# Attention in a decoder trunk: 64 by 64 products for the dilated groups, their weights transposed on TensorE, and a head's values ahead of the next head's scores

## The chip, the core and the metric

The kernel runs on one core of one Trainium2 chip. The metric is the time of one execution on the device in microseconds (us), the median of several runs. The engines are called as in the profile: PE is TensorE (its weight loads are PEld), DVE is VectorE, ACT is ScalarE, POOL is GpSimd, SP is SyncE, which issues most of the loads. PSUM is the memory that PE writes its products to.

## The reference, cut to what matters

A trunk of two layers over 256 tokens of width 1024: layer 0 mixes with a gated short convolution, layer 1 with dilated attention; each is followed by a squared-ReLU MLP (4096 wide) and a gated embedding. The change is in the attention of layer 1 alone.

```python
DILATED_PATTERNS = ((128, 1), (512, 4), (2048, 16))   # window, dilation: groups 0, 1, 2

def dilated_attention_mixer(h, positions, w_qkv, w_o):
    b_, s_, _ = h.shape
    g_, hh, dh = N_ATTN_GROUPS, ATTN_HEADS_PER_GROUP, ATTN_HEAD_DIM   # 3, 8, 128
    qkv = (h @ w_qkv).reshape(b_, s_, 3, g_ * hh, dh)
    q = partial_rotary(qkv[:, :, 0], positions).reshape(b_, s_, g_, hh, dh)
    k = partial_rotary(qkv[:, :, 1], positions).reshape(b_, s_, g_, hh, dh)
    v = qkv[:, :, 2].reshape(b_, s_, g_, hh, dh)
    outs, lses = [], []
    for g, (window, dilation) in enumerate(DILATED_PATTERNS):
        o_g, lse_g = dilated_window_attention(q[:, :, g], k[:, :, g], v[:, :, g], window, dilation)
        outs.append(o_g)
        lses.append(lse_g)
    weights = jax.nn.softmax(jnp.stack(lses, axis=0), axis=0)
    o = jnp.sum(weights[..., None] * jnp.stack(outs, axis=0), axis=0)
    return o.reshape(b_, s_, hh * dh).astype(h.dtype) @ w_o
```

A query of group g sees the keys at most `window` back whose distance is a multiple of `dilation`, itself among them. Weighting the three groups by the softmax of their log-sums is the same as one softmax over the keys of all three groups together, and so the kernel computes it: one row of scores for each query, over the keys of group 0, 1 and 2.

## The kernel before, in words

The program is a list (`make_plan`, line 139) of products and steps, and TensorE's work is issued in the order of that list. A product is one 128-row piece of a weight matrix against the activations; weights come from memory in slabs of up to eight 128 by 128 pieces, and each slab is split into two parts (`whi` on ACT, line 357; `wlo` on DVE, by the helper of line 296), since every product of f32 values is made of three products of rounded ones (`fp32r`). Slabs are split up to five ahead of their use. All products of weights run in `block` (line 393).

The 256 tokens stand in the order of `residue_order` in layer 1: token t at (t mod 4) * 64 and on, so that each run of 64 holds the tokens of one remainder by 4, and inside it runs of 16 hold those of one remainder by 16. Groups 1 (dilation 4) and 2 (dilation 16) therefore only have valid pairs inside a run of 64. A block b is 128 tokens, two such runs.

For each head h of 8, the plan has the products of q and k for the three groups (`qk`, eight k each), with their sums (`add_up`) and rotation (`qk_out`, on POOL for all but the first head's groups), then the products of v for all three groups (`v`, eight k). Between these stand the steps of the head before, in `make_plan` at lines 199 to 206: `scores` after `qk(h, 0)`, `turn` after `qk(h, 2)`, `values` after six of eight k of `v(h)`. For head 0 (`late`) they stand one place later. After the last head, lines 208 to 216 put its three steps between the products of `w_o`, of which k = 0 to 7 stand for the heads' outputs.

- `scores` (line 674): for each block, group 0 as three rounded products over all 256 keys (line 681), groups 1 and 2 each as one plain f32 product of the block's 128 queries with its own 128 keys (line 684). The row of 512 scores is masked and its maximum taken on DVE (line 687), and made into weights on ACT (lines 691, 693).
- `turn` (line 695): the weights must stand with the keys in the partitions. Group 0's 256 columns are transposed on TensorE (line 708), then split in two parts. Those of groups 1 and 2 are transposed on DVE in blocks of 32 by 32: the blocks on the diagonal in one go (line 701), their neighbours within a run of 64 in four more (line 704).
- `v_out` (line 662): the values leave PSUM scaled: group 0 in two parts (lines 668, 669), groups 1 and 2 in one copy of 256 columns (line 670) into `v12`.
- `values` (line 711): group 0 as six rounded products (line 718), then groups 1 and 2 as one plain f32 product for each block and group (line 724), all added into one PSUM bank of 128 by 256; the output is split in two parts (lines 735, 736).

PSUM tiles come from one pool of eight buffers (`bank`, or a `psum.tile` directly); the activations of this stage come from the pools `act` (13 buffers) and `pair` (20).

Of the kernel before, what the change touches and what calls it, by code (L numbers as in the profile page):

```python
# [15 lines left out]
P = 128  # L16
S = 256
# [121 lines left out]
def make_plan():  # L139
# [27 lines left out]
    def mix(key, j, ks):  # L167
        return [("n", key, k, 2 * j + i, ("o", j), i, "y") for k in ks for i in (0, 1)]
# [9 lines left out]
    def qk(h, g, ks):  # L178
        return [
            ("w" if h else "n", "qkv", k, (i, g, h), ("qk", h, g), i, "x3") for k in ks for i in (0, 1)  # L180
        ]

    def v(h, ks):
        return [("t", "v", k, h, ("v", b, h), b, "x3") for k in ks for b in (0, 1)]
# [11 lines left out]
    def sums(h, g):  # L196
        return [("do", "add_up", ("qk", h, g)), ("do", "qk_out", h, g)]

    for h in range(1, HEADS):

        late, steps = h == 1, [[("do", what, h - 1)] for what in ("scores", "turn", "values")]
        plan += qk(h, 0, range(NK)) + ([("do", "values", 0)] if h == 2 else []) + sums(h, 0)
        plan += [("do", "qk_split", 0)] if late else steps[0]
        plan += qk(h, 1, range(NK)) + sums(h, 1) + qk(h, 2, range(NK)) + steps[late ^ 1] + sums(h, 2)
        plan += v(h, range(3)) + [("do", "qk_split", h)] + v(h, range(3, 6)) + steps[2 - late]
        plan += v(h, range(6, NK)) + [("do", "v_out", h)]

    last = HEADS - 1
    plan += [x for k in (0, 1, 2) for j in range(NP) for x in mix("w_o", j, (k,))]
    plan.append(("do", "scores", last))  # L210
    plan += [x for k in (3, 4) for j in range(NP) for x in mix("w_o", j, (k,))]
    plan.append(("do", "turn", last))
    plan += [x for j in range(NP) for x in mix("w_o", j, (5,))]
    plan.append(("do", "values", last))
# [40 lines left out]
def tile_trunk(ctx: ExitStack, tc: tile.TileContext, plan, slabs, ap, out):  # L255
# [36 lines left out]
    def flat(t):  # L292
        return t.rearrange("p i s -> p (i s)")
# [285 lines left out]

    def masks_load():  # L580
        for b in (0, 1):
            mask[b] = apool.tile([P, 512], F32, tag="act", name=f"mask{b}")
            nc.sync.dma_start(mask[b], ap["mask"][:, b, :])

    def conv(c):
# [75 lines left out]

    def v_out(head):

        v0, v12 = act(f"v0_{head}", F32R), act(f"v12_{head}")
        for b in (0, 1):
            p, r = flat(close(("v", b, head))), rstd[3][:, b : b + 1]
            hi, lo = v0[:, b, :P], v0[:, b, P:]
            nc.scalar.activation(hi, p[:, :P], AF.Copy, scale=r)
            nc.vector.scalar_tensor_tensor(lo, p[:, :P], r, f32(hi), ALU.mult, ALU.subtract)
            nc.scalar.activation(v12[:, b, :], p[:, P : GROUPS * P], AF.Copy, scale=r)  # L670
        cur["v", head] = v0, v12


    def scores(head):
        weights = cur["pr", head] = pair(f"sm{head}", dtype=F32)[2]
        for b in (0, 1):
            own = slice(b * P, (b + 1) * P)
            ps = psum.tile([P, 512], F32, tag="ps", name=f"sc{head}_{b}")
            hi, lo, _ = state["qk"][head]
            for n, (q, k) in enumerate(((hi, hi), (hi, lo), (lo, hi))):  # L680
                nc.tensor.matmul(ps[:, :S], q[:, 0, own], k[:, 1, :], start=n == 0, stop=n == 2)  # L681
            for g in (1, 2):
                t = cur["qk", head, g]
                nc.tensor.matmul(ps[:, (g + 1) * P : (g + 2) * P], t[:, 0, own], t[:, 1, own], start=True, stop=True)  # L684
            sm = flat(weights[:, b])
            stats = [spool.tile([P, 1], F32, tag=f"st{n}_{b}", name=f"st{n}_{head}_{b}") for n in range(3)]
            nc.vector.tensor_tensor_reduce(
                out=sm, in0=ps, in1=mask[b], op0=ALU.add, op1=ALU.max, scale=SCALE, scalar=NEG, accum_out=stats[0]
            )
            nc.vector.tensor_scalar(stats[1], stats[0], -1.0, None, ALU.mult)  # L690
            nc.scalar.activation(sm, sm, AF.Exp, bias=stats[1], accum_out=stats[2])
            nc.vector.reciprocal(stats[2], stats[2])
            nc.scalar.activation(sm, sm, AF.Copy, scale=stats[2])

    def turn(head):

        sm = cur.pop(("pr", head))
        t = cur["pT12", head] = act(f"pT12_{head}")  # L700
        nc.vector.transpose(t, sm[:, :, 1, :])
        for q in range(4):
            rows, cols = (slice(n * 32, (n + 1) * 32) for n in (q, q ^ 1))
            nc.vector.transpose(t[cols, :, rows], sm[rows, :, 1, cols])
        ps = bank(f"tp{head}")
        for b in (0, 1):
            for n in (0, 1):
                nc.tensor.transpose(ps[:, n, b * P : (b + 1) * P], sm[:, b, 0, n * P : (n + 1) * P], ident)
        split_into("pT", head, ps)

    def values(head):
        ps = bank(f"o{head}")
        v0, v12 = cur.pop(("v", head))
        hi, lo, _ = state["pT"].pop(head)
        for kb in (0, 1):
            vhi, vlo = v0[:, kb, :P], v0[:, kb, P:]
            for n, (a, b) in enumerate(((vhi, hi), (vhi, lo), (vlo, hi))):
                nc.tensor.matmul(  # L718
                    ps[:, 0, :], a, b[:, kb, :], start=kb == 0 and n == 0, stop=False, skip_group_check=True
                )  # L720
        t = cur.pop(("pT12", head))
        for b in (0, 1):
            for g in (0, 1):
                nc.tensor.matmul(  # L724
                    ps[:, 0, b * P : (b + 1) * P],
                    v12[:, b, g * P : (g + 1) * P],
                    t[:, b, g * P : (g + 1) * P],
                    start=False,
                    stop=g == 1,
                    skip_group_check=True,  # L730
                )
        if head % 2 == 0:
            state["y"][head // 2] = pair(f"y{head // 2}")
        hi, lo = (t[:, head % 2, :] for t in state["y"][head // 2][:2])
        nc.scalar.activation(hi, ps[:, 0, :], AF.Copy)
        nc.vector.tensor_tensor(lo, ps[:, 0, :], f32(hi), ALU.subtract)
# [116 lines left out]
def masks():  # L853

    import numpy as np

    t = np.argsort([residue_order(t) for t in range(S)])
    m = np.full((P, 2, 512), NEG, np.float32)
    for b in range(2):
        q = t[b * P : (b + 1) * P, None]  # L860
        for keys, to, window, step in (
            (t, slice(0, S), 128, 1),
            (t[b * P : (b + 1) * P], slice(S, S + P), 512, 4),
            (t[b * P : (b + 1) * P], slice(S + P, S + 2 * P), 2048, 16),
        ):
            d = q - keys[None]
            m[:, b, to][(d >= 0) & (d <= window) & (d % step == 0)] = 0.0
    return m


# [56 lines left out]
```

## Time and profile before

| | |
|---|---|
| median of 3 runs | 777.29 us (777.19 to 777.32) |
| the profiled execution | 777.36 us, its span 775.5 us |
| granted TensorE clock, mean | 0.998 |
| first to last `scores` (start of line 684) | 349.6 to 543.3 us of the span |
| last `values` (start of line 724) | 554.0 us |

The span is the time from the first to the last instruction in the trace; some 1.9 us of the execution lie around it. In the profile's page the busy times count each engine by itself. Matmuls overlap, so that a busy PE says that something was always under way, not how much fits in. Rows of a timeline give the start, the time from the first start to the last end, engine, line, operation, tiles, shape (stationary rows*columns, then the moving operand) and the count. Rows of one tile give the shortest, median and longest duration in nanoseconds. Rows of waits give the one that waited, the one it waited for, the sum in us, how often and the longest.

### The profile page before, as it was taken

The numbers are of one execution on the slowest core, as the hardware profiler recorded it, in microseconds if no ns is written. First come the engines' busy times: TensorE is split into PE (matmuls) and PEld (weight loads), VectorE is DVE, ScalarE is ACT, GpSimd is POOL, SyncE is SP. The second block draws the span as 40 slices with busy tenths as digits, with TensorE's granted clock in tenths as the row PEclk, the third lists the DMA queues.
The fourth block names the chain that finished last, engine by engine and source line by source line (L and its number), as shares of the span: only waits on it lengthen the run. The fifth ranks groups of instructions, "written<-read, shape, count | busy, mean of one in ns | idle before, by whom it ended". The sixth has DMA issues, their size and how long they took to land.

```text
span 775.5 us, 12403 instructions
## 1 busy us (share of the span) xinstructions
PE 766.9 (99%) x4780; PEld 696.3 (90%) x4780; DVE 595.5 (77%) x863; ACT 439.4 (57%) x677; POOL 167.1 (22%) x110
## 2 busy tenths in 40 slices
PE   9999999999999999999999999999999999999996
PEld 8998998888888899989999989989988888888885
DVE  6898779898566668789789889887798887555664
ACT  7655565565444446557655655655665555444454
POOL 0000000000000000078867867865000000000002
PEclk9999999999999999999999999999999999999999
DMA  8965655655565554654546445456465655555521
GB/s 313 301 192 187 187 184 180 195 187 191 190 188 190 191 190 138 210 182 157 170 150 183 158 152 188 150 161 208 135 211 181 190 188 188 188 188 191 190 93 54
DMA packets 42538, 140.95 MB, mean 182 GB/s; under 512 B 4848, under 2 KB 6128, under 8 KB 42480
## 3 DMA queue, kind: packets, MB, share of 16 engines
q1 hardware_dynamic: 41904, 139.52, 55.9%
q8 instruction: 37, 0.61, 0.3%
q10 hardware_dynamic: 576, 0.66, 0.3%
q14 instruction: 21, 0.17, 0.1%
HBM read 139.10 MB, written 1.05 MB: 181 GB/s over the span
## 4 chain that ended last, share of the span: by engine, by line
PE 97%; issue 1%; DMA 1%; DVE 0%; POOL 0%; SPq 0%; POOLq 0%; DVEq 0%; ACT 0%
PE acc_u L393 23%; PE acc_d L393 23%; PE acc_qk L393 17%; PE acc_v L393 9%; PE acc_o L393 6%; PE acc_g L393 5%; PE acc_B L393 3%; PE acc_C L393 3%; PE acc_X L393 3%; PE o L724 1%; PE sc L684 1%; PE acc_p L393 1%; PE o L718 1%; PE sc L681 1%; DMA pt<-in_pT 1%
## 5 line engine op out<-in xcount | busy, mean ns | idle before, releaser
L296 DVE TENSOR_TENSOR wlo<-raw,whi 128x1024 fp32r<-128x1024 f32 (+2 forms) x277 | 353.2, 1280 | 125.6 <-ACT whi L357 122.7
L357 ACT ACTIVATE whi<-raw 128x1024 fp32r<-128x1024 f32 (+2 forms) x277 | 278.2, 1007 | 214.3 <-PE acc_d L393 77.1
L393 PE MATMUL acc_d<-u,whi 128*128 128x512 f32 x512 | 160.8, 395 | 0.0
L393 PE MATMUL acc_u<-x,whi 128*128 128x512 f32 x512 | 160.8, 395 | 0.0
L393 PE MATMUL acc_qk<-x,whi 128*128 128x512 f32 (+1 forms) x432 | 134.5, 368 | 0.0
L393 PEld LDWEIGHTS acc_d<-u,wlo 128*128 128x128 f32 x512 | 96.2, 188 | 22.7
L393 PEld LDWEIGHTS acc_u<-x,wlo 128*128 128x128 f32 x512 | 96.2, 188 | 22.5
L463 POOL TENSOR_TENSOR n<-v,power 128x2 f32<-128x2 f32 (+1 forms) x6 | 3.9, 650 | 517.1 <-DVE v L488 512.6
L393 PE MATMUL acc_qk<-x,wlo 128*128 128x256 f32 x384 | 108.0, 281 | 0.0
L393 PE MATMUL acc_u<-x,wlo 128*128 128x256 f32 x512 | 101.2, 278 | 0.0
L393 PE MATMUL acc_d<-u,wlo 128*128 128x256 f32 x512 | 100.9, 278 | 0.0
L393 PEld LDWEIGHTS acc_qk<-x,whi 128*128 128x128 f32 x432 | 78.0, 189 | 13.6
L650 POOL TENSOR_TENSOR rot<-qk,sinr 16x512 f32<-16x512 f32 x44 | 78.5, 1785 | 3.0
L393 PEld LDWEIGHTS acc_d<-u,whi 128*128 128x128 f32 x512 | 78.0, 189 | 0.0
L393 PEld LDWEIGHTS acc_u<-x,whi 128*128 128x128 f32 x512 | 78.0, 189 | 0.0
L393 PEld LDWEIGHTS acc_qk<-x,wlo 128*128 128x128 f32 x384 | 72.6, 189 | 0.0
L393 PE MATMUL acc_v<-whi,x 128*128 128x384 f32 x256 | 69.0, 340 | 0.0
L647 POOL TENSOR_TENSOR qk<-qk,cosr 128x512 f32<-128x512 f32 x22 | 37.4, 1698 | 51.4 <-DVE qk L413 41.0
L393 PEld LDWEIGHTS acc_v<-whi,x 128*128 128x128 f32 x256 | 46.6, 188 | 0.0
L393 PE MATMUL acc_o<-y,whi 128*128 128x256 f32 x256 | 46.3, 283 | 0.0
L393 PE MATMUL acc_v<-wlo,x 128*128 128x384 f32 x128 | 42.9, 335 | 0.0
L656 POOL TENSOR_TENSOR qk<-qk,rot 48x512 f32<-48x512 f32 x22 | 42.3, 1924 | 1.7
(176 smaller groups left out, 1036.2 us busy)
## 6 DMA issues: line engine op xcount, KB each, us to landing
raw<-in_w SPq DMA_DIRECT2D x230, 512.0 KB, 4.0
raw<-in_w SPq DMA_DIRECT2D x32, 384.0 KB, 3.1
raw<-in_w SPq DMA_DIRECT2D x10, 256.0 KB, 5.0
h<-in_xT SPq DMA_DIRECT2D x4, 256.0 KB, 5.0
mask<-in_mask SPq DMA_DIRECT2D x2, 256.0 KB, 4.3
gain<-in_gain SPq DMA_DIRECT2D x2, 256.0 KB, 4.3
out<-htg SPq DMA_DIRECT2D x2, 256.0 KB, 2.1
raw<-in_w ACTq DMA_DIRECT2D x2, 128.0 KB, 3.6
```

The lines of the kernel that those rows point to most:

```text
L296: nc.vector.tensor_tensor(out, a, f32(b), ALU.subtract)
L357: nc.scalar.activation(hi[:, :width], t[:, :width], AF.Copy)
L393: nc.tensor.matmul(to, a, b, start=n == 0 and name not in opened, stop=n == len(products) - 1 and left[name, half if kind == "n" else 0] == 0,
L463: nc.gpsimd.tensor_tensor(y, v, power[:, : v.shape[1]], ALU.pow)
L647: engine.tensor_tensor(t, p, both(cosr), ALU.mult)
L650: engine.tensor_tensor(r[dst : dst + 16], p[src : src + 16], sinr[src : src + 16].unsqueeze(1).to_broadcast([16, 2, S]), ALU.mult,)
L656: engine.tensor_tensor(t[:48], t[:48], r[:48], ALU.add)
L681: nc.tensor.matmul(ps[:, :S], q[:, 0, own], k[:, 1, :], start=n == 0, stop=n == 2)
L684: nc.tensor.matmul(ps[:, (g + 1) * P : (g + 2) * P], t[:, 0, own], t[:, 1, own], start=True, stop=True)
L718: nc.tensor.matmul(ps[:, 0, :], a, b[:, kb, :], start=kb == 0 and n == 0, stop=False, skip_group_check=True)
L724: nc.tensor.matmul(ps[:, 0, b * P : (b + 1) * P], v12[:, b, g * P : (g + 1) * P], t[:, b, g * P : (g + 1) * P], start=False, stop=g == 1, ...
```

## The change

In groups 1 and 2 only pairs within a run of 64 tokens are computed. `scores` makes one f32 product of 64 queries by 64 keys for each block, group and run r, into a row of 256 + 128 columns: for run 0 the group 1 scores stand ahead of those of group 2, for run 1 the other way about. These products stand ahead of the three of group 0, and both blocks' PSUM banks are taken first. The masks and the softmax go over 384 columns in place of 512. `turn` transposes all three 128-column pieces of a block on TensorE, in two banks: six transposes in place of four and five on DVE, with one more copy on ACT. Since each query's 128 columns hold both groups, `v_out` lays out the values to match, in eight copies of 64 by 128 on ACT, some of them into the other half of the partitions. `values` then has one product over 128 keys (64 of each group) for each run of 64 queries, cut into two of 64 output rows. In the plan `values` of head h-1 is no step of its own any more but the first thing in `scores` of head h (the last head's `values` stays a step), `turn` and `scores` keep their places, and in the products of `w_o` the last `scores` comes one k sooner.

```diff
--- before.py
+++ after.py
@@ -198,17 +198,16 @@
 
     for h in range(1, HEADS):
 
-        late, steps = h == 1, [[("do", what, h - 1)] for what in ("scores", "turn", "values")]
-        plan += qk(h, 0, range(NK)) + ([("do", "values", 0)] if h == 2 else []) + sums(h, 0)
-        plan += [("do", "qk_split", 0)] if late else steps[0]
-        plan += qk(h, 1, range(NK)) + sums(h, 1) + qk(h, 2, range(NK)) + steps[late ^ 1] + sums(h, 2)
-        plan += v(h, range(3)) + [("do", "qk_split", h)] + v(h, range(3, 6)) + steps[2 - late]
+        late, scores, turn = h == 1, [("do", "scores", h - 1)], [("do", "turn", h - 1)]
+        plan += qk(h, 0, range(NK)) + sums(h, 0) + ([("do", "qk_split", 0)] if late else scores)
+        plan += qk(h, 1, range(NK)) + sums(h, 1) + qk(h, 2, range(NK)) + (scores if late else turn) + sums(h, 2)
+        plan += v(h, range(3)) + [("do", "qk_split", h)] + v(h, range(3, 6)) + (turn if late else [])
         plan += v(h, range(6, NK)) + [("do", "v_out", h)]
 
     last = HEADS - 1
-    plan += [x for k in (0, 1, 2) for j in range(NP) for x in mix("w_o", j, (k,))]
+    plan += [x for k in (0, 1) for j in range(NP) for x in mix("w_o", j, (k,))]
     plan.append(("do", "scores", last))
-    plan += [x for k in (3, 4) for j in range(NP) for x in mix("w_o", j, (k,))]
+    plan += [x for k in (2, 3, 4) for j in range(NP) for x in mix("w_o", j, (k,))]
     plan.append(("do", "turn", last))
     plan += [x for j in range(NP) for x in mix("w_o", j, (5,))]
     plan.append(("do", "values", last))
@@ -579,7 +578,7 @@
 
     def masks_load():
         for b in (0, 1):
-            mask[b] = apool.tile([P, 512], F32, tag="act", name=f"mask{b}")
+            mask[b] = apool.tile([P, S + P], F32, tag="act", name=f"mask{b}")
             nc.sync.dma_start(mask[b], ap["mask"][:, b, :])
 
     def conv(c):
@@ -661,31 +660,46 @@
 
     def v_out(head):
 
+
         v0, v12 = act(f"v0_{head}", F32R), act(f"v12_{head}")
         for b in (0, 1):
-            p, r = flat(close(("v", b, head))), rstd[3][:, b : b + 1]
+            p, scale = flat(close(("v", b, head))), rstd[3][:, b : b + 1]
             hi, lo = v0[:, b, :P], v0[:, b, P:]
-            nc.scalar.activation(hi, p[:, :P], AF.Copy, scale=r)
-            nc.vector.scalar_tensor_tensor(lo, p[:, :P], r, f32(hi), ALU.mult, ALU.subtract)
-            nc.scalar.activation(v12[:, b, :], p[:, P : GROUPS * P], AF.Copy, scale=r)
+            nc.scalar.activation(hi, p[:, :P], AF.Copy, scale=scale)
+            nc.vector.scalar_tensor_tensor(lo, p[:, :P], scale, f32(hi), ALU.mult, ALU.subtract)
+            for r in (0, 1):
+                own, other = (slice(n * 64, (n + 1) * 64) for n in (r, 1 - r))
+                for g, to in ((1, own), (2, other)):
+                    nc.scalar.activation(
+                        v12[to, b, r * P : (r + 1) * P], p[own, g * P : (g + 1) * P], AF.Copy, scale=scale[own]
+                    )
         cur["v", head] = v0, v12
 
 
+
     def scores(head):
+
+        if head:
+            values(head - 1)
         weights = cur["pr", head] = pair(f"sm{head}", dtype=F32)[2]
+        ps = [psum.tile([P, 512], F32, tag="ps", name=f"sc{head}_{b}") for b in (0, 1)]
+        for b in (0, 1):
+            for g in (1, 2):
+                t = cur["qk", head, g]
+                for r in (0, 1):
+                    of, at = slice(b * P + r * 64, b * P + (r + 1) * 64), S + (g - 1 ^ r) * 64
+                    nc.tensor.matmul(
+                        ps[b][r * 64 : (r + 1) * 64, at : at + 64], t[:, 0, of], t[:, 1, of], start=True, stop=True
+                    )
         for b in (0, 1):
             own = slice(b * P, (b + 1) * P)
-            ps = psum.tile([P, 512], F32, tag="ps", name=f"sc{head}_{b}")
             hi, lo, _ = state["qk"][head]
             for n, (q, k) in enumerate(((hi, hi), (hi, lo), (lo, hi))):
-                nc.tensor.matmul(ps[:, :S], q[:, 0, own], k[:, 1, :], start=n == 0, stop=n == 2)
-            for g in (1, 2):
-                t = cur["qk", head, g]
-                nc.tensor.matmul(ps[:, (g + 1) * P : (g + 2) * P], t[:, 0, own], t[:, 1, own], start=True, stop=True)
-            sm = flat(weights[:, b])
+                nc.tensor.matmul(ps[b][:, :S], q[:, 0, own], k[:, 1, :], start=n == 0, stop=n == 2)
+            sm, p = flat(weights[:, b])[:, : S + P], ps[b][:, : S + P]
             stats = [spool.tile([P, 1], F32, tag=f"st{n}_{b}", name=f"st{n}_{head}_{b}") for n in range(3)]
             nc.vector.tensor_tensor_reduce(
-                out=sm, in0=ps, in1=mask[b], op0=ALU.add, op1=ALU.max, scale=SCALE, scalar=NEG, accum_out=stats[0]
+                out=sm, in0=p, in1=mask[b], op0=ALU.add, op1=ALU.max, scale=SCALE, scalar=NEG, accum_out=stats[0]
             )
             nc.vector.tensor_scalar(stats[1], stats[0], -1.0, None, ALU.mult)
             nc.scalar.activation(sm, sm, AF.Exp, bias=stats[1], accum_out=stats[2])
@@ -694,19 +708,16 @@
 
     def turn(head):
 
-
-
         sm = cur.pop(("pr", head))
+        ps = [bank(f"tp{head}_{n}") for n in (0, 1)]
+        for b in (0, 1):
+            for n in range(3):
+                nc.tensor.transpose(
+                    ps[n // 2][:, n % 2, b * P : (b + 1) * P], sm[:, b, n // 2, n % 2 * P : (n % 2 + 1) * P], ident
+                )
+        split_into("pT", head, ps[0])
         t = cur["pT12", head] = act(f"pT12_{head}")
-        nc.vector.transpose(t, sm[:, :, 1, :])
-        for q in range(4):
-            rows, cols = (slice(n * 32, (n + 1) * 32) for n in (q, q ^ 1))
-            nc.vector.transpose(t[cols, :, rows], sm[rows, :, 1, cols])
-        ps = bank(f"tp{head}")
-        for b in (0, 1):
-            for n in (0, 1):
-                nc.tensor.transpose(ps[:, n, b * P : (b + 1) * P], sm[:, b, 0, n * P : (n + 1) * P], ident)
-        split_into("pT", head, ps)
+        nc.scalar.activation(t[:, :, :P], ps[1][:, 0, :].rearrange("p (b q) -> p b q", b=2), AF.Copy)
 
     def values(head):
         ps = bank(f"o{head}")
@@ -719,14 +730,16 @@
                     ps[:, 0, :], a, b[:, kb, :], start=kb == 0 and n == 0, stop=False, skip_group_check=True
                 )
         t = cur.pop(("pT12", head))
-        for b in (0, 1):
-            for g in (0, 1):
+        for n in range(4):
+            q, b, r = slice(n * 64, (n + 1) * 64), n // 2, n % 2
+            for m in (0, 1):
+                to = slice(m * 64, (m + 1) * 64)
                 nc.tensor.matmul(
-                    ps[:, 0, b * P : (b + 1) * P],
-                    v12[:, b, g * P : (g + 1) * P],
-                    t[:, b, g * P : (g + 1) * P],
+                    ps[to, 0, q],
+                    v12[:, b, r * P + m * 64 : r * P + (m + 1) * 64],
+                    t[:, b, r * 64 : (r + 1) * 64],
                     start=False,
-                    stop=g == 1,
+                    stop=n == 3,
                     skip_group_check=True,
                 )
         if head % 2 == 0:
@@ -855,16 +868,18 @@
     import numpy as np
 
     t = np.argsort([residue_order(t) for t in range(S)])
-    m = np.full((P, 2, 512), NEG, np.float32)
+    m = np.full((P, 2, S + P), NEG, np.float32)
     for b in range(2):
         q = t[b * P : (b + 1) * P, None]
-        for keys, to, window, step in (
-            (t, slice(0, S), 128, 1),
-            (t[b * P : (b + 1) * P], slice(S, S + P), 512, 4),
-            (t[b * P : (b + 1) * P], slice(S + P, S + 2 * P), 2048, 16),
-        ):
-            d = q - keys[None]
-            m[:, b, to][(d >= 0) & (d <= window) & (d % step == 0)] = 0.0
+        for r, rows in enumerate((slice(0, 64), slice(64, P))):
+            own = t[b * P : (b + 1) * P][rows]
+            for keys, at, window, step in (
+                (t, 0, 128, 1),
+                (own, S + r * 64, 512, 4),
+                (own, S + (1 - r) * 64, 2048, 16),
+            ):
+                d = q[rows] - keys[None]
+                m[rows, b, at : at + len(keys)][(d >= 0) & (d <= window) & (d % step == 0)] = 0.0
     return m
 
 
```

## The prediction

> **What bounds the kernel now.** I read the page first, then the waits of PE alone, then one head's stretch of the attention stage by windows, then the PE timeline where the changed lines stand.
>
> ```profile
> span 775.5 us, 12403 instructions
> PE 766.9 (99%) x4780; PEld 696.3 (90%) x4780; DVE 595.5 (77%) x863; ACT 439.4 (57%) x677; POOL 167.1 (22%) x110
> ...
> PE 97%; issue 1%; DMA 1%; DVE 0%; POOL 0%; SPq 0%; POOLq 0%; DVEq 0%; ACT 0%
> ```
>
> PE is busy for 99% of the span, and the chain that ended last is PE for 97%. The waits of PE by themselves are two starts of the program and one more:
>
> ```profile
> PE warm L523 <- DVE power L519: 1.0, 1, 1.0
> PE acc_p L393 <- ACT whi L357: 0.2, 1, 0.2
> ```
>
> Nothing in the attention stage makes PE wait. So the time moves only by what the change adds to or takes from PE's own work, as long as no new wait appears. One head's period, from its first score to the next head's (start, end, length, then busy time of each engine):
>
> ```profile
> 395.50:424.10 28.60, 28.60 (x177) 26.58 (x176) 24.92 (x34) 17.00 (x30) 21.31 (x12) 1.00 0.53 161
> ```
>
> PE 28.6 of 28.6 us, at the full granted clock (1.00); DVE 24.9, ACT 17.0, POOL 21.3. DVE is the nearest behind.
>
> **The PE work that is replaced.** A busy PE says little about the cost of one matmul, since they overlap: the cost is the distance from one start to the next. Rows of the PE timeline (start, time from the first start to the last end, count):
>
> ```profile
> 289.39 0.51 PE L478 MATMUL ssq<-ones,tot 128*128 128x2 f32 x4
> 289.76 0.36 PE L393 MATMUL acc_g<-x,wlo 128*128 128x256 f32 x1
> ...
> 395.49 0.51 PE L681 MATMUL sc<-qk 128*128 128x256 f32 x3
> 395.83 0.61 PE L684 MATMUL sc<-qk 128*128 128x128 f32 x4
> 396.20 0.61 PE L681 MATMUL sc<-qk 128*128 128x256 f32 x3
> 396.64 0.60 PE L684 MATMUL sc<-qk 128*128 128x128 f32 x4
> 397.00 0.36 PE L393 MATMUL acc_qk<-x,wlo 128*128 128x256 f32 x1
> 397.20 0.40 PE L393 MATMUL acc_qk<-x,whi 128*128 128x512 f32 x1
> ...
> 408.19 0.60 PE L708 MATMUL tp<-ident,sm 128*128 128x128 f32 x4
> 408.55 0.42 PE L393 MATMUL acc_v<-whi,x 128*128 128x384 f32 x1
> ...
> 415.59 1.05 PE L724 MATMUL o<-pT,v 128*128 128x128 f32 x8
> 416.40 0.42 PE L393 MATMUL acc_v<-whi,x 128*128 128x384 f32 x1
> ```
>
> and the durations of single ones, with their weight loads:
>
> ```profile
> L684 PEld LDWEIGHTS sc<-qk x64: 187/192/193, 349.5 to 543.1; 128*128 128x128 f32 x64
> L684 PE MATMUL sc<-qk x64: 270/275/276, 349.6 to 543.3; 128*128 128x128 f32 x64
> ...
> L724 PE MATMUL o<-pT,v x64: 271/275/276, 365.9 to 554.0; 128*128 128x128 f32 x64
> ...
> L708 PE MATMUL tp<-ident,sm x32: 271/272/273, 357.1 to 549.4; 128*128 128x128 f32 x32
> ```
>
> The code calls line 684 32 times (8 heads, 2 blocks, 2 groups) and the trace has 64: a plain f32 product is two loads and two matmuls. A transpose is one (4 calls a head, 32 in all). Four of line 684 last 0.61 us, one 0.275, so three distances are 0.335 and **one instruction costs 0.11 us**. Line 724: (1.05 - 0.275) / 7 = 0.11. Line 708: (0.60 - 0.272) / 3 = 0.109. The four at line 478 have 2 moving columns and not 128, and still hold PE for 0.37 us (289.39 to 289.76), as four of line 684 do (395.83 to 396.20). So at 128 moving columns it is the load of 128 stationary columns, not the moving side, that sets the 0.11: halving the moving side alone would bring nothing, and the change halves both.
>
> Before, per head: 8 instructions of line 684 and 8 of line 724, 16 x 0.11 = 1.76 us. The products of group 0 (lines 681, 718) stay.
>
> **After**, per head: scores 2 blocks x 2 groups x 2 halves = 8 products, values 4 quarters x 2 halves = 8 products, so 32 instructions of 64 stationary and 64 moving columns. No row of before has fewer than 128 stationary columns. The upper bound for one is 0.11, if size does not count. If it follows the columns, 0.055. The lower bound is the smallest distance that the rows hold: the fourth of line 684 begins at 396.64 + 3 x 0.11 = 396.97 and the next line 393 at 397.00, 0.03 later (that one's follower then comes 0.20 later, so nothing was gained there; it shows only that starts can lie so near). What speaks for the low end is the order of the new loops: the index that goes round fastest is the half (outputs in partitions 0 to 63, then 64 to 127), so that neighbours share neither stationary columns nor output partitions, and two can be in the array side by side: 0.055 / 2 = 0.0275, which is next to the 0.03. I take 0.03: 32 x 0.03 = 0.96, **-0.80 us a head, -6.4 for 8**.
>
> The Trainium skill says in "TensorEngine Tiling (Array Packing)", Key Properties, that tiles load and multiply in parallel; 64-column tiles would then give up to 2x over 0.055, which is 0.0275. No run here shows it yet.
>
> **Added transposes.** The third 128-column piece of each block now goes through TensorE: 2 more a head at 0.109 beside the 4 of line 708, 16 in all, **+1.74 us**, all of it on PE and nothing hides it.
>
> **Changes of width.** PE goes from products over 128 columns to ones over 64 and back. With values of head h-1 directly ahead of scores of head h, and the 64-column scores first, that is one region a head: 8 score regions (the first with no values) and the last head's values alone, 9 regions, 18 changes. Before shows none. Lower bound 0: the next load runs ahead as it does between kinds now. Upper bound: the next load starts only after the last matmul ended, 0.275 - 0.11 = 0.165 of overlap lost, and the load of 0.19 is bare too, 0.355. I take 0.165, from line 684, since a load needs only its operand and may be ahead: **18 x 0.165 = +2.97 us** (bounds 0 and 6.4).
>
> "TensorEngine Tiling (Array Packing)", Key Properties, of the Trainium skill speaks against this change here: switching the tiling mode drains the TensorE. It gives no price; 0.165 stands in its place, and without the drain the sum would be 2.97 us lower.
>
> **What lies beside PE.** These rows price the other engines:
>
> ```profile
> L668 ACT ACTIVATE v<-acc_v,n x16: 367/367/369, 332.3 to 533.3; 128x128 fp32r<-128x128 f32 x16
> L670 ACT ACTIVATE v<-acc_v,n x16: 466/471/476, 338.2 to 535.4; 128x256 f32<-128x256 f32 x16
> ...
> L735 ACT ACTIVATE y<-o x8: 384/384/387, 367.0 to 554.3; 128x256 fp32r<-128x256 f32 x8
> ```
> ```profile
> L704 DVE STREAM_TRANSPOSE pT<-sm 32x64 f32<-32x64 f32 x32 | 7.6, 237 | 0.8
> L701 DVE STREAM_TRANSPOSE pT<-sm 128x512 f32<-128x512 f32 x8 | 5.7, 710 | 7.5 <-ACT sm L693 7.5
> ```
> ```profile
> ACT whi L357 <- PE acc_qk L393: 28.2, 18, 2.5
> ```
>
> ACT: 8 copies of 64 by 128 in `v_out` at the 0.367 of line 668 in place of 2 at 0.471, +2.0 us, and one copy of `pT12` at 0.384: +2.4 a head, 19.4 of 28.6. The narrower softmax (384 for 512 columns) takes some back. ACT's weight splits now wait for PE to free a buffer (28.2 us over the qk stages), so they are early and can slip by that. The copies also hold the two banks of v longer; with eight banks they are next needed only behind the following head's `qk` of group 0 and its scores. DVE loses 0.71 + 4 x 0.237 = 1.66 us a head. Cost 0; if that cover were gone, PE would wait up to 2.4 us a head. POOL's rotation is the nearest deadline:
>
> ```profile
> 418.87 2.16 POOL L656 TENSOR_TENSOR qk<-qk,rot 48x512 f32<-48x512 f32 x1
> ```
>
> It ends at 421.03, and the scores that read it start at 424.1. In the new order the read comes 0.35 us earlier within `scores` (the group 0 products now follow) but some 1.2 us later by the values ahead of it: still 3 us. `values` itself moves from 415 to the next scores at 424; its operands wait longer in their buffers, and nothing on PE asks for its output until `w_o`. `turn` has the same place behind `scores`, 11 us on. For head 0 it comes sooner:
>
> ```profile
> 355.69 1.34 ACT L693 ACTIVATE sm<-sm,st 128x512 f32<-128x512 f32 x2 [0.32 <-DVE st L692]
> ```
> ```profile
> 357.14 0.60 PE L708 MATMUL tp<-ident,sm 128*128 128x128 f32 x4
> ```
>
> The softmax ends at 357.03, 0.11 us ahead of the transposes. It is four ACT passes and two of DVE over a quarter fewer columns, so it ends earlier, and I price this at 0; at worst 0.5 us once. The two masks are a quarter smaller, loaded well before use: 0.
>
> **The sum.** -6.40 + 1.74 + 2.97 = -1.7 us. The profiled execution took 777.36 us (span 775.5, 1.9 outside it); the median shown is 777.29. Forecast **775.6 us**, -0.22%. A measurement of this kernel can tell about 0.2% (1.55 us) from no change, so the forecast lies on that edge: the two unseen prices decide.
>
> **The rivals.**
>
> 1. *The halves go one after another.* Each 64-column instruction then costs 0.055: 32 x 0.055 = 1.76, as much as before; transposes and changes of width stay: +4.7, **782.0 us**. For it: every row of before shows PE taking one product after another, and starts 0.03 apart gained nothing there. Against it: only the disjoint columns. The change turns to a loss where an instruction costs over (14.08 - 4.71) / 256 = 0.037 us. Chance 0.25.
> 2. *The change of width costs its upper bound.* 18 x 0.355 = 6.4, with 0.03 for an instruction: +1.7, 779.0 us. The prices between this and none are the range of the forecast itself (772.6 to 779.0). Chance of the upper end 0.04.
> 3. *Load and product of one instruction cannot overlap.* 0.055 + 0.055 = 0.11 each, 3.52 a head, +14.1 +1.74 +2.97: **796 us**. Against it: in the window above PE and PEld are busy together (28.6 and 26.6 of 28.6), over the same 128 rows. Chance 0.05. "TensorE: Matmul & The Clock Gate", The mechanism, in the Trainium skill says that a load overlaps a running matmul only where the row groups differ, which would be this case; those two busy times disagree with it.
> 4. *A wait takes the place of the work saved*, most likely at the last head, where `turn` and `values` are one k of `w_o` apart (2.9 us), or behind ACT's eight copies: up to 0.5 us there, 2.4 a head if it were ACT, 775 to 795. Chance 0.03.
>
> That the products stay at full width cannot be: the slices are 64 wide.
>
> **How the numbers follow.** Forecast and its own range: 0.67, of which 0.42 have a change of width under 0.17 us (faster by over 0.2%), 0.21 between 0.17 and 0.35 (within 0.2%), 0.04 above or with dearer instructions. Rival 1: 0.25, of which 0.02 near enough to the break-even to be the same. Rivals 3 and 4: 0.08, slower. Faster 0.42, same 0.23, slower 0.35. The likeliest case's own range is 772.6 to 779.0; the range for 8 in 10 reaches below for 0.0275 an instruction with no change of width to pay (32 x 8 x 0.0025 = 0.6 less, 772.0, little likely) to 772.4, and above to rival 1 with a little more than 0.165 a change, 783.
>
> **What would show it.** In the changed profile the forms of 64 columns of `sc` and `o` give it at once: 16 of them in about 0.48 us and pairs that start together are the forecast; 0.88 us is rival 1; 1.76 is rival 3. The first instruction after each change of width shows the drain as a longer distance. `tp` must have 48 matmuls at 0.109. A line of PE in the waits of the attention stage, or a head's period that shrinks by less than PE's rows say, would be rival 4. My forecast falls if PE shows no overlap of the halves.

## The result, and the profile after

The changed kernel takes 782.21 us (median, 781.58 to 782.91), the kernel before beside it 777.24: a ratio of 1.0065, 95% interval 1.0047 to 1.0082. It is slower by 5.0 us, where 1.7 us less was forecast. The number is next to that of the first rival (782.0), but the profile shows another mechanism, so that the agreement is chance. The page of the changed kernel, its busy engines and its chain:

```profile
span 780.1 us, 12716 instructions
...
PE 768.1 (98%) x4924; PEld 694.4 (89%) x4924; DVE 581.8 (75%) x823; ACT 452.7 (58%) x733; POOL 165.0 (21%) x110
...
PE 94%; DVE 3%; issue 2%; ACT 1%; POOL 0%; POOLq 0%; DVEq 0%
```

The span grew by 4.6 us, PE's busy time by 1.2: PE stands idle for 3.4 us more. In the chain DVE has 3% and ACT 1%, where both had 0% before. First the steady heads, where the 64-wide products went as forecast. PE timeline of the changed kernel at one head (line 729 is group 0's values, 737 the 64-wide values, 691 the 64-wide scores, 698 group 0's scores):

```profile
399.49 0.87 PE L729 MATMUL o<-pT,v 128*128 128x256 f32 x6
400.29 0.69 PE L737 MATMUL o<-pT,v 128*64 128x64 f32 x16
400.80 0.64 PE L691 MATMUL sc<-qk 128*64 128x64 f32 x16
401.37 0.98 PE L698 MATMUL sc<-qk 128*128 128x256 f32 x6
402.18 0.28 PE L392 MATMUL acc_qk<-x,wlo 128*128 128x256 f32 x1
```

with the duration of one from the rows of the tile, and the head's window:

```profile
L691 PEld LDWEIGHTS sc<-qk x128: 133/138/138, 349.2 to 544.1; 128*64 128x64 f32 x128
L691 PE MATMUL sc<-qk x128: 222/222/271, 349.2 to 544.1; 128*64 128x64 f32 x128
```

```profile
400.80:429.34 28.54, 28.54 (x200) 26.09 (x198) 21.83 (x29) 18.35 (x37) 21.42 (x12) 1.00 0.54 165
```

Sixteen scores last 0.64 us and one 0.222, so fifteen distances are 0.42: 0.028 us each. Taken one by one, their starts come in pairs, 6 to 7 ns and then 51 to 52 ns apart. The halves do run side by side. A head takes 28.54 us, where it took 28.6: no loss in the steady state, but a gain of only 0.1 us.

The loss is in one place. The waits of PE, then its timeline there:

```profile
PE tp L715 <- ACT sm L707: 3.8, 1, 3.8
```

```profile
356.71 0.34 PE L392 MATMUL acc_v<-whi,x 128*128 128x384 f32 x1
360.85 1.05 PE L715 MATMUL tp<-ident,sm 128*128 128x128 f32 x6 [3.80 <-ACT sm L707]
361.66 0.43 PE L392 MATMUL acc_v<-whi,x 128*128 128x384 f32 x1
361.92 0.50 PE L392 MATMUL acc_v<-wlo,x 128*128 128x384 f32 x1
362.21 0.84 PE L392 MATMUL acc_v<-whi,x 128*128 128x384 f32 x2
362.85 0.53 PE L392 MATMUL acc_v<-wlo,x 128*128 128x384 f32 x1
```

Head 0's transposes wait for the softmax; from the last product of v ahead of them to their start it is 4.14 us, where 0.17 is usual: 3.97 us lost. And what follows is slow: products of v start 0.32 us apart (362.21 to 362.85 is two), where 0.173 is usual. The windows of this stretch give the granted clock in the column after the engines (1.00 is the full clock):

```profile
356.90:360.80 3.90, 0.15 (x1) 0.00 (x0) 3.90 (x5) 0.61 (x2) 3.76 (x3) 1.00 0.30 88
360.80:362.20 1.40, 1.35 (x8) 1.15 (x9) 1.40 (x1) 1.40 (x3) 1.32 (x2) 0.91 0.09 35
362.20:365.60 3.40, 3.40 (x13) 3.40 (x13) 3.39 (x4) 2.13 (x6) 1.23 (x1) 0.54 0.50 124
365.60:368.00 2.40, 2.40 (x16) 2.09 (x15) 2.23 (x5) 2.36 (x6) 0.00 (x0) 1.00 0.77 241
```

After the idle stretch PE ran 3.4 us at about half the clock: some 1.6 us more (ten products of v at about 0.15 us extra). The transposes take 0.81 us up to the next product of v, in place of 0.57, mostly since the weights of block 1 come at 361.31 only. Wait, transposes and clock together are 5.8 us; the other heads give back what leaves 5.0 in all, some 0.8.

Why is the softmax late? Its last pass on ACT waits for DVE's reciprocals, 4.5 us later than before (355.69 there):

```profile
360.00 0.21 DVE L706 RECIPROCAL st<-st 128x1 f32<-128x1 f32 x2
```

```profile
360.19 1.12 ACT L707 ACTIVATE sm<-sm,st 128x384 f32<-128x384 f32 x2 [3.30 <-DVE st L706]
```

From there the trail goes back over three engines. ACT after `v_out` of head 0, in the changed kernel:

```profile
338.08 3.00 ACT L673 ACTIVATE v<-acc_v,n 64x128 f32<-64x128 f32 x8 [1.80 <-DVE v L669]
341.10 0.66 ACT L411 ACTIVATE qk<-acc_qk 128x256 f32<-128x256 f32 x2
```

and in the kernel before:

```profile
338.25 0.84 ACT L670 ACTIVATE v<-acc_v,n 128x256 f32<-128x256 f32 x2 [1.80 <-DVE v L669]
338.97 0.38 ACT L412 ACTIVATE qk<-acc_qk 128x256 f32<-128x256 f32 x1
```

The eight copies take 3.0 us, the two took 0.84, and the first sum of head 1 behind them in ACT's queue is 2.1 us later. DVE needs it. DVE in the changed kernel:

```profile
341.52 0.76 DVE L412 TENSOR_TENSOR qk<-acc_qk,qk 128x256 f32<-128x256 f32 x2 [1.22 <-ACT qk L411]
342.45 1.75 DVE L295 TENSOR_TENSOR qk<-qk,qk 128x512 fp32r<-128x512 f32 x1 [0.18 <-ACT qk L429]
344.12 4.01 DVE L295 TENSOR_TENSOR wlo<-raw,whi 128x768 fp32r<-128x768 f32 x2
348.06 0.74 DVE L412 TENSOR_TENSOR qk<-acc_qk,qk 128x256 f32<-128x256 f32 x2
348.72 4.85 DVE L295 TENSOR_TENSOR wlo<-raw,whi 128x768 fp32r<-128x768 f32 x2
353.50 0.55 DVE L701 CUSTOM_DVE_ANT_0 sm<-sc,mask 128x384 f32<-128x384 f32 x1
```

and before:

```profile
340.40 0.74 DVE L413 TENSOR_TENSOR qk<-acc_qk,qk 128x256 f32<-128x256 f32 x2
341.06 0.67 DVE L296 TENSOR_TENSOR qk<-qk,qk 128x512 fp32r<-128x512 f32 x1
341.66 1.81 DVE L296 TENSOR_TENSOR wlo<-raw,whi 128x768 fp32r<-128x768 f32 x2
...
345.07 1.75 DVE L296 TENSOR_TENSOR wlo<-raw,whi 128x768 fp32r<-128x768 f32 x1 [0.31 <-ACT whi L357]
347.83 1.23 DVE L296 TENSOR_TENSOR wlo<-raw,whi 128x1024 fp32r<-128x1024 f32 x1 [1.01 <-ACT whi L357]
350.26 0.69 DVE L687 CUSTOM_DVE_ANT_0 sm<-sc,mask 128x512 f32<-128x512 f32 x1 [1.20 <-PE sc L684]
```

The order of DVE's instructions is the same (a row of two splits is named by its first; the row of 4.85 us holds one of 768 and one of 1024 columns). The sum of q and k begins 1.1 us later, and the rounding of q and k and the four splits behind it cost 1.75 + 4.01 + 4.85 = 10.6 us in place of 0.67 + 1.81 + 1.75 + 1.23 = 5.5. POOL's rotation of head 1 runs beside them, but it does so in the kernel before too. What differs is which of the two engines starts first. POOL's first instruction, in the changed kernel and in the one before:

```profile
342.36 1.30 POOL L646 TENSOR_TENSOR qk<-qk,cosr 128x512 f32<-128x512 f32 x1 [6.67 <-DVE qk L412]
```

```profile
341.21 3.42 POOL L647 TENSOR_TENSOR qk<-qk,cosr 128x512 f32<-128x512 f32 x1 [5.37 <-DVE qk L413]
```

Before, DVE's rounding (341.06) stood 0.15 us ahead of it: DVE took its usual 0.67 us and POOL 3.42. In the changed kernel DVE waits 0.18 us more for ACT's part of the rounding, which the copies have delayed, and POOL is 0.09 us ahead: POOL takes 1.30 us, DVE's rounding 1.75, and the two engines then take turns. The traces bear this out over the attention stage (300 to 560 us). Of the 198 weight splits that started while no POOL instruction was under way, in the two kernels and in the runs below with the copies moved, with the copies alone and with the splits moved, none took over 1.1 times its usual length; of the 252 that started during one, 234 did. No run tests this start by itself.

The masked maximum, which before waited for PE and had DVE idle for 1.2 us, starts 3.2 us later, and the reciprocals, behind one more split and one more rounding, 4.5 us later.

### The profile page after: what moved, and what is told of

Same layout as the page of the kernel before. It is cut to its first block, busy times and chain, and to the rows that moved or that the text cites. A ratio compares the mean times of both kernels' runs of the same rounds, so it can differ in the third digit from the quotient of the medians.

```text
span 780.1 us, 12716 instructions
## 1 busy us (share of the span) xinstructions
PE 768.1 (98%) x4924; PEld 694.4 (89%) x4924; DVE 581.8 (75%) x823; ACT 452.7 (58%) x733; POOL 165.0 (21%) x110
## 4 chain that ended last, share of the span: by engine, by line
PE 94%; DVE 3%; issue 2%; ACT 1%; POOL 0%; POOLq 0%; DVEq 0%
PE acc_u L392 23%; PE acc_d L392 23%; PE acc_qk L392 15%; PE acc_v L392 7%; PE acc_o L392 6%; PE acc_g L392 5%; PE acc_B L392 3%; PE acc_C L392 3%; PE acc_X L392 3%; PE acc_p L392 1%; DVE wlo L295 1%; PE sc L698 1%; PE o L729 1%; PE tp L715 1%; PE o L737 1%
## 5 line engine op out<-in xcount | busy, mean ns | idle before, releaser
L295 DVE TENSOR_TENSOR wlo<-raw,whi 128x1024 fp32r<-128x1024 f32 (+2 forms) x277 | 361.5, 1311 | 157.6 <-ACT whi L356 155.2
L655 POOL TENSOR_TENSOR qk<-qk,rot 48x512 f32<-48x512 f32 x22 | 40.4, 1838 | 1.7
```

Of the source, the lines that this page charges most:

```text
L295: nc.vector.tensor_tensor(out, a, f32(b), ALU.subtract)
L655: engine.tensor_tensor(t[:48], t[:48], r[:48], ALU.add)
```

## The experiments

Theory A is the trail above: ACT's copies, DVE's splits, the maximum, PE's wait, the half clock. Theory B: the wait comes from the new order inside `scores`. Theory C: the time goes in the changes of width in every head.

**The copies of head 0 moved.** `v_out` of head 0 leaves its eight copies to a step behind head 0's transposes; nothing else differs from the changed kernel.

```diff
+            if head:
+                v12_copy(v12, p, scale, b)
+            else:
+                cur["v12", b] = v12, p, scale, b
...
-        plan += v(h, range(3)) + [("do", "qk_split", h)] + v(h, range(3, 6)) + (turn if late else [])
+        plan += v(h, range(3)) + [("do", "qk_split", h)] + v(h, range(3, 6)) + (turn + [("do", "v12_out")] if late else [])
```

> The changed kernel, but head 0's eight copies of v12 stand behind head 0's transposes and not in v_out. Theory A (the eight ACT copies of head 0 hold up head 1's first sum by 2.1 us, DVE's weight splits then run beside POOL's rotation, the masked maximum of head 0 starts 3.2 us late, PE waits 3.97 us at head 0's transposes and then runs 3.4 us at half the clock, some 1.8 us more): the wait is gone, 782.2 - 5.7 = 776.5 us, between 775.9 and 777.2. Theory B (the wait comes from scores itself, since the 64-wide products of both blocks now stand ahead of group 0's and block 0's row is complete later): the wait stays, 782 us. Theory C (the time goes in the changes of width in all heads, and the wait is made up later): over 780 us.

Measured: 775.86 us, the kernel before beside it 776.99; ratio 0.9985 (0.9975 to 0.9994). Its maximum and its transposes of head 0:

```profile
350.24 0.56 DVE L711 CUSTOM_DVE_ANT_0 sm<-sc,mask 128x384 f32<-128x384 f32 x1 [1.56 <-PE sc L708]
```

```profile
356.67 0.82 PE L725 MATMUL tp<-ident,sm 128*128 128x128 f32 x6
```

The maximum waits for PE again, the transposes wait for nothing. The total is 0.6 us below the 776.5 expected. B falls, and C as the cause of the loss; what a change of width costs comes further below. It ran again later, with the last experiment below:

> e1_copies_later once more, beside e8_group0_first on one chip: 775.9 us, 1.1 us under the kernel before.

Measured: 775.72 beside 776.85, ratio 0.9986 (0.9977 to 0.9995). This version beats both kernels, by 1.1 us (0.14%) against the one before.

**The copies alone, in the kernel before.**

```diff
-            nc.scalar.activation(v12[:, b, :], p[:, P : GROUPS * P], AF.Copy, scale=r)
+            if head:
+                nc.scalar.activation(v12[:, b, :], p[:, P : GROUPS * P], AF.Copy, scale=r)
+                continue
+            for own in (slice(0, 64), slice(64, P)):
+                for g in (0, 1):
+                    at = slice(g * P, (g + 1) * P)
+                    nc.scalar.activation(v12[own, b, at], p[own, P + g * P : P + (g + 1) * P], AF.Copy, scale=r[own])
```

> The kernel before, but head 0's two copies of 128 by 256 into v12 are made as eight of 64 by 128, same layout; nothing else. Theory A: head 0's transposes, which had 0.11 us to spare, wait 3 to 5 us and PE runs at half clock after: 782 to 784 us. Theory B or C: nothing on PE changes, 777.3 us.

Measured: 782.33 us beside 776.99, ratio 1.0067 (1.0052 to 1.0082): the whole loss, without any 64-wide product. PE's waits (one of 3.4 us and a short one, for the weights of block 1), and the window behind them:

```profile
PE tp L714 <- ACT sm L699: 3.5, 2, 3.4
```

```profile
361.60:365.00 3.40, 3.40 (x13) 3.40 (x12) 3.25 (x8) 2.12 (x4) 1.28 (x1) 0.50 0.39 116
```

**The wait filled.** Products that nothing reads stand ahead of head 0's transposes.

```diff
+        if not head:
+            fill = bank("fill")
+            for n in range(18):
+                nc.tensor.matmul(fill[:, 0, :P], ones, ones, start=True, stop=True)
```

> The changed kernel with 18 products of ones by ones (36 instructions of 0.107 us, 3.9 us, into a bank that nothing reads) ahead of head 0's transposes. If the half clock after the wait is from PE's idleness, PE stays at full clock and the wait is merely filled: 782.2 - 1.8 = 780.4 us. If the lower clock has another cause, or costs nothing: 782.2 us, or more by what does not fit in the wait.

Measured: 779.92 us (before: 776.99, ratio 1.0038, 1.0023 to 1.0053). The transposes start at 360.87, as late as in the changed kernel, but the clock holds:

```profile
356.85 4.18 PE L714 MATMUL fill<-ones 128*128 128x128 f32 x36
360.87 1.01 PE L719 MATMUL tp<-ident,sm 128*128 128x128 f32 x6
```

```profile
362.20:365.60 3.40, 3.40 (x22) 3.18 (x21) 3.40 (x4) 3.19 (x7) 1.22 (x1) 1.00 0.42 123
```

So the half clock came from PE's idleness. From the first transpose to the next product of q and k it is 2.95 us here and 4.54 in the changed kernel, so that the slow clock costs 1.6 us on top of the wait (1.8 expected). The medians, each against the kernel before beside it, differ by 4.97 - 2.93 = 2.0 us; where the other 0.4 goes isn't shown. With nine products in place of 18:

> As e3_fill_the_wait, but 9 products in place of 18: PE works for 1.9 us of the wait and idles for some 2 us. If the clock falls only after an idle stretch of about the length seen (4 us), it stays full: 780 us, as with the full filling. If 2 us of idleness are enough: 782 us, as without filling.

Measured: 780.34 us (before: 776.82, ratio 1.0048, 1.0033 to 1.0063), the remaining wait and the clock behind it:

```profile
PE tp L719 <- ACT sm L707: 1.8, 1, 1.8
```

```profile
362.20:365.60 3.40, 3.40 (x22) 3.14 (x21) 3.40 (x3) 2.85 (x6) 0.87 (x1) 1.00 0.51 151
```

In this trace an idle stretch of 1.8 us leaves the clock alone; 3.4 (in the kernel before with eight copies) and 3.8 (in the changed kernel) do not. One of the four executions of this run took 781.80 us, though, at a mean clock of 0.995 where the other three have 0.997 to 0.999; it has no trace, and whether the clock fell there after the 1.8 us isn't shown. "TensorE: Matmul & The Clock Gate" in the Trainium skill, Part 1, puts the measure at a window of about 3.4 us. The traces agree in so far as their bound lies between 1.8 and 3.4 us, and the slow stretch of the changed kernel was 3.4 us long (by the windows above, with the slow clock taken as 0.50: 1.4 x 2 x 0.09 + 3.4 x 2 x 0.46).

**The link over DVE.** The eight copies stay where the change put them; two of DVE's splits go behind head 0's maximum: the slabs are split three ahead, not five, during `qk(1, 2)`, and the two are made up inside `scores` of head 0, kept in that order.

```diff
-        plan += qk(h, 1, range(NK)) + sums(h, 1) + qk(h, 2, range(NK)) + (scores if late else turn) + sums(h, 2)
+        plan += qk(h, 1, range(NK)) + sums(h, 1) + [("do", "look", LOOK - 2 if late else LOOK)] + qk(h, 2, range(NK)) + (scores + [("do", "look", LOOK)] if late else turn) + sums(h, 2)
...
+            if look[0] != LOOK:
+                keep(made)
...
+        if not head:
+            split_to(len(parts))
```

> The changed kernel with the eight copies of head 0 where the change put them, but on DVE two weight splits that stood ahead of head 0's masked maximum stand behind it (one directly behind, one behind the reciprocals). Theory A says the chain runs from the copies over DVE's splits beside POOL's rotation to the maximum: the maximum starts by 350.5 us and not 353.5, PE's wait of 3.97 us falls under 0.6 us, the clock stays full, 776 to 777 us. If the copies hold the softmax up on ACT itself and not by way of DVE, the wait stays: 782 us.

Measured: 777.02 us beside 776.82, ratio 1.0002 (0.9993 to 1.0012). The maximum and the first of the two splits behind it:

```profile
349.93 0.56 DVE L705 CUSTOM_DVE_ANT_0 sm<-sc,mask 128x384 f32<-128x384 f32 x1 [1.66 <-PE sc L702]
...
351.35 0.95 DVE L358 TENSOR_TENSOR wlo<-raw,whi 128x768 fp32r<-128x768 f32 x1
```

The wait at the transposes is gone with the copies in place (they still take 3.0 us on ACT, and the rounding of q and k behind them still 1.75 on DVE), so the way led over DVE. It stays 1.2 us above the version with the copies moved; another wait, once, in the scores of head 2, is nearly as long:

```profile
PE sc L694 <- POOL qk L658: 1.1, 1, 1.1
```

**The pairs.** From the version with the copies moved, the loops of `scores` are turned so that one half's eight instructions come first.

```diff
-        for b in (0, 1):
-            for g in (1, 2):
-                t = cur["qk", head, g]
-                for r in (0, 1):
+        for r in (0, 1):
+            for b in (0, 1):
+                for g in (1, 2):
+                    t = cur["qk", head, g]
```

> As e1_copies_later, but in scores the half is the slow index: eight instructions of one half, then eight of the other. If pairs of neighbours in different halves are what makes 64-wide instructions cost 0.029 us, the sixteen cost 0.055 each: 16 x 0.026 x 8 = 3.3 us above e1_copies_later. If the array orders them by itself, or it is the narrower shape alone: the same as e1_copies_later.

Measured: 777.92 us (ratio to before 1.0012, 1.0003 to 1.0022), 2.06 above its base where 3.3 was expected. The sixteen scores:

```profile
394.83 0.92 PE L701 MATMUL sc<-qk 128*64 128x64 f32 x16
395.68 0.97 PE L708 MATMUL sc<-qk 128*128 128x256 f32 x6
```

Within one half, instructions start 58 ns apart; in pairs, 58 ns bring two. That it cost less than expected is seen in the single starts: around the turn from one half to the other, three pairs come 4 to 6 ns apart in every head, so a few of the second half run beside the last of the first. Three pairs save some 3 x 0.054 = 0.16 us of the 0.42 a head that were expected.

**The changes of width.** From the version with the copies moved, the values of head h-1 go back between the products of v.

```diff
-        if head:
-            values(head - 1)
...
-        plan += qk(h, 0, range(NK)) + sums(h, 0) + ([("do", "qk_split", 0)] if late else scores)
+        plan += qk(h, 0, range(NK)) + ([("do", "values", 0)] if h == 2 else []) + sums(h, 0)
+        plan += [("do", "qk_split", 0)] if late else scores
...
-(turn + [("do", "v12_out")] if late else [])
+(turn + [("do", "v12_out")] if late else [("do", "values", h - 1)])
```

> As e1_copies_later, but from head 1 on the values stand where they stood before the change, between the products of v, so that heads 1 to 6 have two regions of 64-wide products each and PE changes width 12 times more. At the 0.17 us a change that the trace of the changed kernel shows (0.14 in, 0.2 out): 12 x 0.17 = +2.0 us above e1_copies_later, 777.9 us. If a change costs nothing and only the narrow shape counts: the same as e1_copies_later.

Measured: 777.95 us (ratio to before 1.0013, 1.0004 to 1.0023), 2.1 above its base: 0.17 us a change, as expected (0.19 if each is taken against the kernel before beside it). The head's window is 28.90 us, 0.36 longer for its two added changes:

```profile
395.28:424.18 28.90, 28.90 (x195) 26.18 (x195) 23.34 (x30) 19.62 (x39) 21.93 (x12) 1.00 0.53 177
```

**What stands ahead of q and k.** In the changed kernel the 512-column products of q and k of groups 1 and 2 start 236 ns apart on average, in a fixed round of 232, 236 and 241; in the kernel before, 230. This takes back some 0.12 us a head. In `scores`, group 0's products go first, then the values of the head before, then the 64-wide scores.

```diff
+        for b in (0, 1):
+            own = slice(b * P, (b + 1) * P)
+            for n, (q, k) in enumerate(((hi, hi), (hi, lo), (lo, hi))):
+                nc.tensor.matmul(ps[b][:, :S], q[:, 0, own], k[:, 1, :], start=n == 0, stop=n == 2)
         if head:
             values(head - 1)
```

> As e1_copies_later, but scores begins with group 0's six products, then come the values of the head before and the 64-wide scores, so that a region of 64-wide products ends with q and k of the next head and not with group 0's products. In e1_copies_later the 512-column products of q and k behind scores lie 236 ns apart, 230 in the kernel before (48 products a head with 512 columns, some 0.12 us a head more with their neighbours). If that is set by what stands directly ahead of them, the distance changes here, by up to 0.1 us a head, 0.9 us in all: 775 or 776.8. If it is set by the kernel's place in memory or the like: as e1_copies_later.

Measured: 775.85 us, ratio 0.9986 (0.9978 to 0.9995): no difference, and the same round of 232, 236 and 241 ns. What stands directly ahead does not set it. Its cause stays open.

## Why the prediction was wrong, step by step

- **An instruction of 64 by 64 at 0.03 us.** Right: 0.029, two in 58 ns, because neighbours lie in different halves. Rival 1 (0.055 each) gave the measured total by chance, and the measured time lies within the range given (772.4 to 783) only since that rival stretched it; the row of the 64-wide forms refutes it.
- **A change of width at 0.165 us.** Right in sum. The starts show 0.14 us into the region (209 ns in place of 118 for the last wide one, 100 in place of 51 between the first pairs) and 0.20 out of it; the run with the values apart gives 0.17. "TensorEngine Tiling (Array Packing)", Key Properties, in the Trainium skill says that the array drains here; the longer distances at both ends fit that, but no row shows the array empty (the first 64-wide product starts 0.21 us after the last wide one, which lasts 0.28).
- **Two more transposes at 0.109 us.** Right: six take 0.57 us of distances, four took 0.355.
- **The sum of the steady heads**, -0.25 us a head. Mis-sized: measured -0.10. Values, scores and changes gave -0.43 (forecast -0.47), the transposes +0.22 as forecast; the slower q and k products, which nobody had asked for, took 0.12 back.
- **Rival 3** (0.11 us, load and product not overlapped) falls with the rows of line 691: a load of 0.138 and a product of 0.222 in one stream of 0.058 us a half. The rule of the Trainium skill that the prediction quotes with it does not hold here as it stands; the same section also lets a load into the background weight buffer run ahead.
- **The step that failed: ACT's eight copies, "Cost 0", and head 0's softmax, priced "at 0; at worst 0.5 us once".** The copies were sized rightly (0.362 us each, 0.367 taken). Their cover was read from the steady heads and from ACT's total slack. But the instruction behind them in head 0 is the sum of head 1's first q and k, and the chain from there leads to head 0's softmax, which ended 0.11 us ahead of the transposes by the prediction's own rows. It asked only whether the softmax had become shorter, not whether it would start on time. The wait is 3.97 us, not 0.5: the 2.1 us on ACT were 1.1 at DVE's sum, then grew to 3.2 at the maximum and 4.5 at the reciprocals, where DVE came behind POOL. Rival 4 named this place, a wait behind ACT's eight copies, but with 0.5 us and a chance of 0.03.
- **The price of a wait.** Rival 4 counted a wait by its own length. Idle for 3.4 and 3.8 us, PE lost more after it, by the clock: 1.6 us in the trace of the changed kernel, 2.0 by the medians.

Without the one wait, the version with the copies moved takes 775.7 to 775.9 us, where 775.6 was forecast. That is closer than the forecast deserves: the kernel before took 776.9 to 777.0 beside it, 0.3 to 0.4 us under the time that the forecast started from. The gain is 1.1 us where 1.7 was forecast, and the slower products of q and k alone take 0.7 back over all heads (131.84 us from start to start in that trace, 131.18 in the kernel before).

## What to carry to other kernels

On an engine that other engines feed, look up for every added instruction what stands directly behind it in its own queue, at the first and the last turn of a loop as well as in the steady ones, and follow that to the next deadline of the bound engine. A slack of a tenth of a microsecond in the trace is a warning, and the question is when the chain begins, not only how long it is. Where DVE and POOL work on the same stretch, look which of them starts first. Where PE is the bound, count a wait like the ones seen here (3.4 and 3.8 us) at its length plus 1.6 to 2 us of half clock, and if the total agrees with a rival, still read the row that the rival stands on.

## What was not expected of the hardware

- The same DVE instruction takes very different times beside POOL: a split of 768 columns 0.94 us in the kernel before, where POOL's first instruction took 3.42 us, and about 2 us (4.01 for two) in the changed kernel, where that one took 1.30. Of the two, the one that started first went at its usual pace and the other paid: with an order turned by some 0.2 us, DVE's rounding and four splits took 5.1 us more.
- After the `scores` of a head the wide products of q and k keep a round of 232, 236 and 241 ns; the next head's group 0 runs at 231 again. The cause is open.
- With one half's eight instructions written ahead of the other's, three pairs still started 4 to 6 ns apart. "TensorE: Matmul & The Clock Gate", The mechanism, in the Trainium skill says that matmuls keep strict order in start and end; in the order of the loops that would allow one pair at the turn. The rows don't name an instruction's half, and the order in which PE was given them isn't shown, so this stays open.
